# Background steps carried on into the next projection, the last shift row turned five steps later, and the first recurrence queued behind that row

## The chip, the cores and the metric

The kernel runs on one core of a Trainium2 chip. The metric is the device time of one launch in microseconds (us), lower is better. Engines are named as the profile names them: PE (TensorE matmuls), PEld (weight loads of TensorE), DVE (VectorE), ACT (ScalarE), POOL (GpSimd) and SP (SyncE, which issues most loads). Each engine works through its own instructions in the order in which they stand in its queue, and waits where an instruction needs something that another engine or a transfer has not delivered.

## The reference, cut to what matters

One decoder block on 512 tokens of width 2048, all in float32. A modulation vector is computed from `c`; the normalised input goes through one wide projection, whose columns feed attention (8 heads) and a gated recurrence, HGRN2 (8 heads).

```python
mod = silu(c) @ w_ada + b_ada
shift1, scale1, gate1, shift2, scale2, gate2 = split(mod, 6)
h = rms_norm(x, norm1_w) * (1 + scale1) + shift1
aq, ak, av, gq, gf, gi, gg = split(h @ w_in, ...)       # 7 parts of 1024 columns
attn = rms_norm(dilated_attention(rope(norm(aq)), rope(norm(ak)), av))
f = lb + (1 - lb) * sigmoid(gf)
hg = rms_norm(hgrn2(silu(gq), f, gi)) * silu(gg)         # 8 heads, a decayed running state
x = x + gate1 * (concat(attn, hg) @ w_out)
h2 = rms_norm(x, norm2_w) * (1 + scale2) + shift2
x = x + gate2 * (square(relu(h2 @ w_ff1)) @ w_ff2)
```

## The kernel before, in words

**Tiles.** Every float32 product is made of three matmuls of 128x512: both operands are split into a rounded part (`hi`, `whi`) and a rest (`lo`, `wlo`). For a weight tile ACT makes `whi` (line 39) and DVE makes `wlo` (line 40). A projection of 512 columns, `project` (L370 and on), runs over 16 steps of the contraction, called k-steps here; each k-step is 12 matmuls into four PSUM banks named `prj`. There are only four such banks, so ACT must copy a bank out (`evac`, copies at L406; `hgrn_q`, copies at L564; `hg_gate`, copies at L705) before the next projection may write to it.

**What runs beside the projections.** Two lists of generators are advanced from within `project`. After each k-step one `tick` (L360) advances the front of `tasks`: a recurrence `hgrn` of four heads with 12 ticks each, or an `attention` of four heads with 25 ticks in all. At the same place `bg_step` (L346) advances the front of `bgw`, at a rate of 2.0 steps per k-step in the first of these projections and 1.85 in the others. A background row is a matrix-vector product on DVE: `gemv` (L116) loads 16 pieces `araw` of 256 KB and adds each, times a scalar, into `acc`, one step per piece; `to_cols` (L139) then adds the two accumulators, yields, and has PE turn the row with four transposes into a bank `pc` (L149), which ACT sums up into columns (L152).

**The place of the change.** The shift vector of the first modulation is applied late: `shift_through(col0)` (L748) computes the row of `shift1 @ w_in` for columns from `col0` and adds it as a bias to values that are already there, the gates `f0` for column 4096 and the queries `hq0` for column 3072. Both rows are background steps of the projection of column 5120 (`hv0`), 32 steps in 16 k-steps, so that the transposes of the row of 3072 come with its last k-step. Then a `while bgw` loop empties the list, `bgw` is filled with `later` (a row for 4608, the four rows of `gate1`, then eight rows of the second modulation), and the first recurrence, which needs `f0`, `hq0` and `hv0`, is put on `tasks`. The projections that follow are, in order, `q0`, `k0_`, `v0`, `hq1`, `hv1`, `q1`, `k1`, `v1` and the two gates; 48 ticks of the recurrence fill exactly the 48 k-steps of `q0`, `k0_` and `v0`, and the attention of the first four heads begins with `hq1`.

**What sets the order.** On PE the order is that of the code (`manual_schedule` for PE). On the other engines a scheduler puts the instructions in order when the program is built, by the order in which the code issues them, with evacuations, weight loads, the decay levels of the recurrence and the softmax (`s_sb`, L474 to L478) put forward (`high_priority`).

**Later stages** are the output projection, the first feed-forward layer, and products of seven half-size blocks for the rest of the feed-forward layers (`product`, L1181 to L1183, whose weights DVE combines at L1149 and splits into `vlo` at L1166).

## Time and profile before

| | us |
|---|---|
| median of 3 timed runs | 2286.12 |
| lowest and highest of them | 2283.48 and 2286.8 |
| profiled execution: its span, the only time the profile gives for it | 2283.5 |
| PE busy in it | 2225.3 |
| DVE busy in it | 1809.0 |
| ACT busy in it | 1098.0 |
| projection of column 5120 (`hv0`), first to last matmul | 187.4 to 240.8 |
| last k-step of `hq1`, last matmul starts | 467.79 |

The profile counts from the first instruction to the last (the span). A row of a timeline gives start, duration, engine, line of the code, operation, "output<-inputs", shape and, in brackets, the idle time before it with what ended that. A row of the waits gives the total, the number and the longest of the waits of one kind. A row of the stretches gives for each engine its busy time and the number of its instructions, then PEclk, the share of the full TensorE clock that was granted, and the share and rate of the DMA engines.

### The profile page before, as it was taken

The page shows a single profiled execution, that of the slowest core. Times are in us where ns is not written, and L with a number is a line of the kernel's source. Part 1 is how long each engine was busy: PE and PEld are TensorE (multiplying, and loading weights), DVE is VectorE, ACT ScalarE, POOL GpSimd, SP SyncE. Part 2 cuts the span into 40 slices and gives each one's busy share as a digit, 9 for nine tenths or more (in the row PEclk, how much of TensorE's full clock was granted, in tenths as well). Part 3 has the DMA queues.
Part 4 walks back from the last instruction along what each step waited for, and adds up shares of the span by engine and source line. Part 5 has one row for each costly group of instructions (what it writes and reads, how often), then busy time and mean ns, then how long its engine had stood idle before and what let it go on. Part 6 is the DMA issues. An engine that isn't in the chain of part 4 may idle for free.

```text
span 2283.5 us, 33098 instructions
## 1 busy us (share of the span) xinstructions
PE 2225.3 (97%) x11769; PEld 1825.0 (80%) x11769; DVE 1809.0 (79%) x2765; ACT 1098.0 (48%) x1950; POOL 443.2 (19%) x664
## 2 busy tenths in 40 slices
PE   4999999999999999999999999999999999999999
PEld 3787877878778888888888888888888888788887
DVE  6999778668786575678658988998897779967878
ACT  5555434433354454447545555565564333343332
POOL 1000022000220000002232323323232222222221
PEclk9999999999999999999999999999999999999999
DMA  9798455546555266847879789789899987998784
GB/s 325 255 333 321 123 183 167 183 154 214 178 166 178 65 204 215 267 126 257 324 274 365 277 308 382 294 294 374 320 331 370 344 312 257 359 349 293 278 296 165
DMA packets 262583, 598.31 MB, mean 262 GB/s; under 512 B 23221, under 2 KB 43969, under 8 KB 262417
## 3 DMA queue, kind: packets, MB, share of 16 engines
q1 hardware_dynamic: 186800, 332.54, 43.5%
q0 software_dynamic: 70720, 254.21, 30.3%
q10 hardware_dynamic: 4896, 9.44, 1.2%
q8 instruction: 93, 1.52, 0.3%
q14 instruction: 74, 0.60, 0.1%
HBM read 518.49 MB, written 77.61 MB: 261 GB/s over the span
## 4 chain that ended last, share of the span: by engine, by line
PE 67%; issue 12%; DMA 11%; DVE 7%; POOL 3%; ACT 1%; SPq 0%; POOLq 0%; DVEq 0%; ACTq 0%
PE prj L198 9%; PE prj L200 9%; PE prj L199 8%; PE f L1183 8%; PE f L1182 8%; PE f L1181 8%; DMA f_lod<-fs 3%; PE f L208 2%; PE f L206 2%; PE f L207 2%; DMA f_hid<-part 2%; PE prj L207 2%; DVE vlo L1166 2%; PE prj L208 2%; DMA araw<-in_w_ada_dram 1%
## 5 line engine op out<-in xcount | busy, mean ns | idle before, releaser
L1165 ACT CAST vhi<-raw 128x1024 fp32r<-128x1024 f32 x392 | 413.5, 1056 | 537.9 <-PE f L1183 420.5
L1166 DVE TENSOR_TENSOR vlo<-raw,vhi 128x1024 fp32r<-128x1024 f32 x392 | 478.1, 1226 | 154.5 <-ACT vhi L1165 153.8
L1182 PE MATMUL f<-vlo,Fh 128*128 128x512 f32 x1376 | 537.7, 391 | 4.2 <-DVE vlo L1166 4.1
L1181 PE MATMUL f<-vhi,Fh 128*128 128x512 f32 x1376 | 536.9, 390 | 0.9 <-ACT vhi L1165 0.9
L1183 PE MATMUL f<-vhi,Fl 128*128 128x512 f32 x1376 | 536.3, 390 | 0.2 <-DMA Fl<-f_lod 0.2
L39 ACT CAST whi<-wraw 128x512 fp32r<-128x512 f32 (+1 forms) x368 | 220.1, 601 | 445.4 <-PE prj L200 296.0
L198 PE MATMUL prj<-whi,hi 128*128 128x512 f32 x896 | 365.1, 408 | 3.8 <-ACT gq L564 2.4
L200 PE MATMUL prj<-whi,lo 128*128 128x512 f32 x896 | 351.3, 392 | 0.0
L199 PE MATMUL prj<-wlo,hi 128*128 128x512 f32 x896 | 350.9, 392 | 0.0
L40 DVE TENSOR_TENSOR wlo<-wraw,whi 128x512 fp32r<-128x512 f32 (+1 forms) x368 | 243.8, 668 | 124.3 <-ACT whi L39 121.6
L129 DVE SCALAR_TENSOR_TENSOR acc<-araw,sc,acc 128x512 f32<-128x512 f32 (+1 forms) x392 | 253.9, 677 | 95.1 <-DMA araw<-in_w_ada_dram 94.0
L1182 PEld LDWEIGHTS f<-vlo,Fh 128*128 128x128 f32 x1376 | 258.8, 188 | 63.2 <-DVE vlo L1166 9.9
L1181 PEld LDWEIGHTS f<-vhi,Fh 128*128 128x128 f32 x1376 | 258.6, 188 | 55.0 <-ACT vhi L1165 1.4
L1183 PEld LDWEIGHTS f<-vhi,Fl 128*128 128x128 f32 x1376 | 258.8, 188 | 54.1 <-DMA Fl<-f_lod 0.6
L1149 DVE TENSOR_TENSOR raw<-raw,raw 128x1024 f32<-128x1024 f32 x224 | 269.4, 1224 | 3.4 <-DMA raw<-in_w_ff_dram 2.9
L198 PEld LDWEIGHTS prj<-whi,hi 128*128 128x128 f32 x896 | 169.0, 189 | 40.0 <-ACT gq L564 3.8
L200 PEld LDWEIGHTS prj<-whi,lo 128*128 128x128 f32 x896 | 169.0, 189 | 37.0 <-DVE lo L240 0.3
L199 PEld LDWEIGHTS prj<-wlo,hi 128*128 128x128 f32 x896 | 169.4, 189 | 32.6 <-DVE wlo L40 0.9
L1127 POOL DMA_DIRECT2D Fh<-f_hid x112 | 79.0, 705 | 428.5 <-PE f L1183 416.2
L208 PE MATMUL f<-hi,wlo 128*128 128x512 f32 x256 | 99.9, 390 | 1.5 <-DVE wlo L40 1.5
L206 PE MATMUL f<-hi,whi 128*128 128x512 f32 x256 | 100.3, 392 | 0.0
L207 PE MATMUL f<-lo,whi 128*128 128x512 f32 x256 | 99.6, 389 | 0.0
(311 smaller groups left out, 2917.2 us busy)
## 6 DMA issues: line engine op xcount, KB each, us to landing
raw<-in_w_ff_dram SPq DMA_DIRECT2D x224, 512.0 KB, 9.2
araw<-in_w_ada_dram SPq DMA_DIRECT2D x384, 256.0 KB, 4.3
Fh<-f_hid POOLq DMA_DIRECT2D x112, 512.0 KB, 6.1
Fl<-f_lod POOLq DMA_DIRECT2D x112, 512.0 KB, 7.1
wraw<-in_w_in_dram SPq DMA_DIRECT2D x104, 512.0 KB, 4.0
Fh<-h_hid POOLq DMA_DIRECT2D x60, 512.0 KB, 6.1
Fl<-h_lod POOLq DMA_DIRECT2D x60, 512.0 KB, 7.2
f_hid<-part POOLq DMA_DIRECT2D x48, 512.0 KB, 7.6
```

The costliest lines, as they stand in the source:

```text
L39: nc.scalar.copy(hi, src)
L40: (eng or nc.vector).tensor_tensor(lo, src, hi.bitcast(F32), op=ALU.subtract)
L129: dve.scalar_tensor_tensor(acc, raw[:, k - k0], vec[:, k:k + 1], acc, op0=ALU.mult, op1=ALU.add)
L198: pe.matmul(banks[ti], lhsT=hi[:, ts], rhs=whi, start=first, stop=False)
L199: pe.matmul(banks[ti], lhsT=hi[:, ts], rhs=wlo, start=False, stop=False)
L200: pe.matmul(banks[ti], lhsT=lo[:, ts], rhs=whi, start=False, stop=last)
L1149: dve.tensor_tensor(dst, a, b, op=ALU.subtract)
L1165: act.copy(hi, src)
L1166: split_done.append(dve.tensor_tensor(lo, src, hi.bitcast(F32), op=ALU.subtract))
L1181: pe.matmul(banks[t], lhsT=fh[u][a][:, ts], rhs=whi[:, a], start=first, stop=False)
L1182: pe.matmul(banks[t], lhsT=fh[u][a][:, ts], rhs=wlo[:, a], start=False, stop=False)
L1183: pe.matmul(banks[t], lhsT=fl[u][a][:, ts], rhs=whi[:, a], start=False, stop=end)
```

## The change

```diff
-    def to_cols(accs, dst):
+    def to_cols(accs, dst, lag=0):
...
             dve.tensor_tensor(accs[0], accs[0], accs[1], op=ALU.add)
-        yield
+        for _ in range(lag + 1):
+            yield
         pc = bank("pc")
...
-        yield from to_cols(gemv.acc, col[:, 0:4])
+        yield from to_cols(gemv.acc, col[:, 0:4], 5 if col0 == 3072 else 0)
...
                 forget(hd, f[h], f[h], col[:, h:h + 1])
+        shift_done.add(col0)
         yield
...
     hv0 = evac(project(5120, tok_mm, 2.0), "gi")
-    while bgw:
-        bg_step()
-    bgw[:] = later
+    bgw.extend(later)
+
+    def until(key):
+        while key not in shift_done:
+            yield
+
+    tasks.append(until(3072))
     tasks.append(hgrn(f0, hq0, hv0, hrs[0]))
```

The row of column 3072 waits five more background steps between its sum on DVE and its transposes on PE. The list is no longer emptied at the end of `hv0`, so these steps fall into `q0`: with 1.85 steps per k-step, the fifth one comes with the third k-step. A task `until` uses up the ticks until then. So on PE the transposes of that row stand three k-steps (36 matmuls) later, the first recurrence begins three ticks later, ends in `hq1` instead of `v0`, and the first attention follows three ticks later, within `hq1` and `hv1`. All background rows of `later` move by five steps, about three k-steps. From `q1` on the recurrence and the attention of the other heads stand where they stood; only the background rows still differ, until they run out. No instruction of computation is added or removed.

ACT, at the end of `hq1`, where the four `prj` banks are copied out as `gq` so that `hv1` can begin. `s_sb` are the exponentials of an attention head, `whi` weight tiles, `qT` transposed queries and keys, `sg` a gate computed from `gq`. Before:

```order
L39 CAST whi<-wraw 128x512 x2
L478 ACTIVATE s_sb,lsum<-s_sb,m 128x512
L564 COPY gq<-prj 128x512
L478 ACTIVATE s_sb,lsum<-s_sb,m 128x384
L478 ACTIVATE s_sb,lsum<-s_sb,m 128x128
L564 COPY gq<-prj 128x512
L478 ACTIVATE s_sb,lsum<-s_sb,m 128x256
L564 COPY gq<-prj 128x512
L568 ACTIVATE sg<-gq 128x512
L39 CAST whi<-wraw 128x512
L564 COPY gq<-prj 128x512
```

The same place of the changed kernel:

```order
L493 COPY p_sb<-pT 128x512 x2
L493 COPY p_sb<-pT 128x256
L565 COPY gq<-prj 128x512
L569 ACTIVATE sg<-gq 128x512
L565 COPY gq<-prj 128x512 x2
L39 CAST whi<-wraw 128x512
L569 ACTIVATE sg<-gq 128x512
L565 COPY gq<-prj 128x512
L457 ACTIVATE qT<-ptq,wcol 128x512 x2
```

The exponentials that stood around the four copies are gone from there; in their place stand the copies of the transposed weights of the same head (`p_sb`), and the next exponentials come behind the copies.

ACT, at the end of `q0`, where the four banks are copied out as `aq`. `f<-pho` copies the output of a recurrence head, `gq,hss` are the four sums of squares of it, `jk` are sums of squares of `aq`. Before:

```order
L687 COPY f<-pho 128x512
L690 ACTIVATE gq,hss<-f 128x128 x4
L39 CAST whi<-wraw 128x512 x3
L406 COPY aq<-prj 128x512
L417 ACTIVATE jk,rs_3201<-aq 128x128
L406 COPY aq<-prj 128x512
L417 ACTIVATE jk,rs_3201<-aq 128x128 x3
L406 COPY aq<-prj 128x512
L417 ACTIVATE jk,rs_3201<-aq 128x128 x4
L406 COPY aq<-prj 128x512
```

The same place of the changed kernel:

```order
L688 COPY f<-pho 128x512
L691 ACTIVATE gq,hss<-f 128x128
L407 COPY aq<-prj 128x512
L691 ACTIVATE gq,hss<-f 128x128 x3
L407 COPY aq<-prj 128x512
L418 ACTIVATE jk,rs_3106<-aq 128x128 x4
L407 COPY aq<-prj 128x512 x2
```

The output of the recurrence head now comes right ahead of the copies, three k-steps later than it did, and its squares stand between them.

DVE, early in the seven-block products of the feed-forward layer, right behind two sums `s` (L1238 before, L1244 after). `raw` is a combination of two weight tiles, `vlo` the rest part that PE waits for. Before:

```order
L1166 TENSOR_TENSOR vlo<-raw_12705,vhi 128x1024
L1149 TENSOR_TENSOR raw_12701<-raw_12709,raw_12701 128x1024
L1166 TENSOR_TENSOR vlo<-raw_12699,vhi 128x1024
L1149 TENSOR_TENSOR raw_12703<-raw_12711,raw_12703 128x1024
L1149 TENSOR_TENSOR raw_12705<-raw_12713,raw_12705 128x1024
L1149 TENSOR_TENSOR raw_12709<-raw_12717,raw_12709 128x1024
L1166 TENSOR_TENSOR vlo<-raw_12701,vhi 128x1024
L1149 TENSOR_TENSOR raw_12699<-raw_12715,raw_12699 128x1024
L1149 TENSOR_TENSOR raw_12711<-raw_12719,raw_12711 128x1024
L1149 TENSOR_TENSOR raw_12713<-raw_12721,raw_12713 128x1024
L1166 TENSOR_TENSOR vlo<-raw_12703,vhi 128x1024
```

The same place of the changed kernel:

```order
L1172 TENSOR_TENSOR vlo<-raw_12705,vhi 128x1024
L1155 TENSOR_TENSOR raw_12701<-raw_12709,raw_12701 128x1024
L1155 TENSOR_TENSOR raw_12703<-raw_12711,raw_12703 128x1024
L1172 TENSOR_TENSOR vlo<-raw_12699,vhi 128x1024
L1155 TENSOR_TENSOR raw_12705<-raw_12713,raw_12705 128x1024
L1155 TENSOR_TENSOR raw_12709<-raw_12717,raw_12709 128x1024
L1172 TENSOR_TENSOR vlo<-raw_12701,vhi 128x1024
L1155 TENSOR_TENSOR raw_12711<-raw_12719,raw_12711 128x1024
L1172 TENSOR_TENSOR vlo<-raw_12703,vhi 128x1024
```

The fourth `vlo` of this piece now stands behind five combinations instead of seven; the second stands behind two instead of one.

## The prediction

> **What bounds the kernel now.** I read the page first. Its first lines give the span and the busy time of each engine, and its list of the chain that ended last shows whose work makes up the end.

> ```profile
> span 2283.5 us, 33098 instructions
> PE 2225.3 (97%) x11769; PEld 1825.0 (80%) x11769; DVE 1809.0 (79%) x2765; ACT 1098.0 (48%) x1950; POOL 443.2 (19%) x664
> PE 67%; issue 12%; DMA 11%; DVE 7%; POOL 3%; ACT 1%; SPq 0%; POOLq 0%; DVEq 0%; ACTq 0%
> ```

> PE is busy all but 58 us. An edit that keeps its instructions can win only in those 58 us, and in stretches where PE runs slowly while it counts as busy. So the second view is the waits of PE (total, number, longest):

> ```profile
> PE pc L149 <- DVE acc L143: 4.9, 1, 4.9
> PE f L1182 <- DVE vlo L1166: 4.1, 7, 1.5
> PE prj L198 <- ACT gq L564: 2.4, 1, 2.4
> PE prj L198 <- ACT gg L705: 1.3, 1, 1.3
> ```

> Those of the first 40 us are left out here, since the change does not reach them. The 4.9 us are the transposes of the row of column 4096, inside `hv0`; I find them at 208.9 to 214.1 us. The 2.4 us end at a copy of `gq`, between `hq1` and `hv1`. The third view is the table of stretches around these waits. Behind the core's stretch stand busy times, PEclk, DMA share and rate:

> ```profile
> 208.90:214.10 5.20, 0.39 (x2) 0.00 (x0) 5.20 (x10) 0.62 (x1) 0.00 (x0) 0.74 1.06 388
> 214.10:218.20 4.10, 4.05 (x12) 3.38 (x13) 3.70 (x7) 2.84 (x7) 0.00 (x0) 0.50 1.05 387
> 467.80:470.50 2.70, 0.37 (x2) 0.00 (x0) 2.19 (x9) 1.26 (x4) 0.00 (x0) 1.00 0.03 9
> 470.50:474.20 3.70, 3.62 (x8) 2.47 (x9) 0.82 (x3) 3.70 (x12) 0.00 (x0) 0.54 0.00 0
> 809.50:813.50 4.00, 4.00 (x23) 3.44 (x24) 2.02 (x5) 3.91 (x8) 0.00 (x0) 1.00 0.47 131
> 1965.80:1969.20 3.40, 3.40 (x10) 2.66 (x9) 3.40 (x7) 0.00 (x0) 0.00 (x0) 0.50 1.04 399
> ```

> After the waits of 4.9 and 2.4 us the clock stood near half; after the 1.3 us for `gg` it did not fall. So a long wait costs more than itself.

> **The place of the edit itself: nothing to win.** Did PE wait for the row that is now turned later?

> ```profile
> 240.84 0.39 PE L200 MATMUL prj<-whi,lo 128*128 128x512 f32 x1
> 241.07 0.60 PE L149 MATMUL pc<-ident,acc 128*128 128x128 f32 x4
> 231.40 0.69 DVE L143 TENSOR_TENSOR acc<-acc 128x512 f32<-128x512 f32 x1
> ```

> No: the transposes start 0.23 us behind the last matmul of `hv0`, the normal pace, and their sum had been ready on DVE since 232. Moving them by 36 matmuls is worth 0. The distance from them to the first recurrence matmuls stays at two k-steps, so ACT and DVE have as long as before to finish the queries between them. The 4.9 us wait lies ahead of the first moved instruction; DVE, ACT, SP and PE have the same order up to there, so it stays, with its slow 4.1 us. The five lag steps issue nothing. The background rows keep their distance from their own loads; on SP the longest run of `araw` loads between two weight loads grows from seven to eleven in the new order, which the four buffers of weight loads cover as long as DVE frees the `araw` buffers in time (the slower rival below is the case where it doesn't). The three ticks are taken up by spare ones: the 25 ticks of the attention, from the fourth k-step of `hq1` on, end in the 12th of the 16 of `hv1`.

> What changes is what stands beside what at the ends of projections.

> **Term 1, the end of `hq1`.** PE, then ACT, then DVE:

> ```profile
> 467.79 0.39 PE L208 MATMUL prj<-hi,wlo 128*128 128x512 f32 x1
> 470.58 0.65 PE L198 MATMUL prj<-whi,hi 128*128 128x512 f32 x1 [2.41 <-ACT gq L564]
> 476.91 0.39 PE L199 MATMUL prj<-wlo,hi 128*128 128x512 f32 x1
> 477.82 0.39 PE L200 MATMUL prj<-whi,lo 128*128 128x512 f32 x1
> 478.05 1.25 PE L490 MATMUL pT<-ident,s_sb 128*128 128x128 f32 x10
> 469.24 0.72 ACT L478 ACTIVATE s_sb<-s_sb,m 128x512 f32<-128x512 f32 x1 [3.35 <-DVE m L477]
> 469.96 0.56 ACT L564 COPY gq<-prj 128x512 f32<-128x512 f32 x1
> 473.90 0.58 ACT L564 COPY gq<-prj 128x512 f32<-128x512 f32 x1
> 464.99 0.75 DVE L129 SCALAR_TENSOR_TENSOR acc<-araw,sc,acc 128x512 f32<-128x512 f32 x1 [1.16 <-DMA araw<-in_w_ada_dram]
> 465.66 1.92 DVE L474 SCALAR_TENSOR_TENSOR s_sb<-pscore,rs,lnc_sb 128x512 f32<-128x512 f32 x4
> ```

> ACT stood 3.35 us at an exponential that waited for DVE's maximum, and the first `gq` copy was queued behind it. DVE was late because a background piece ahead of the softmax had waited for its load. From 467.79 to 478.05 there are 25 matmul steps. At 0.2275 us each (476.91 to 477.82 is four) they take 5.69; they took 10.26. The loss is 4.6 us: 2.4 of waiting, 1.7 by the clock (3.7 us at 0.54), 0.5 of further waits for copies.

> In the changed kernel the scores of that head come at k-step 59 of the count from `q0` and those of the next at 65, while the copies come at 64, so no exponential is ahead of them. Does the new queue hold PE? Three `p_sb` copies stand ahead, and eight transposes `ptq` stand on PE before `hv1`:

> ```profile
> 478.77 1.34 ACT L492 COPY p_sb<-pT 128x512 f32<-128x512 f32 x3
> 454.52 0.60 PE L454 MATMUL ptq<-ident,aq 128*128 128x128 f32 x4
> 455.32 0.48 PE L206 MATMUL prj<-hi,whi 128*128 128x512 f32 x1
> ```

> From the start of the last k-step: `pT` began 1.0 earlier, and by the row 478.77 its copies are done 2.06 after its start, at 1.05. Then a copy (0.57), `sg`, two copies (0.47 apart, by the rows of term 2), a cast, `sg`, a copy (0.57). With 0.72 for each `sg` and the cast, what the exponential of the same width took at 469.24, the fourth bank is free at 5.3. PE ends the k-step (12 steps) at 2.7, does `ptq` in 0.8 to 0.9 and wants the fourth bank nine steps later, at 5.6. It does not wait. **-4.6 us**, between -2.4 and -4.6.

> **Term 2, the end of `q0`.** There ACT now has the output of a recurrence head just ahead of the copies. Rows of ACT, and last the wait of PE's matmuls of line 198 for `aq` (total, number):

> ```profile
> 407.89 0.59 ACT L687 COPY f<-pho 128x512 f32<-128x512 f32 x1 [1.13 <-PE pho L685]
> 408.51 0.31 ACT L690 ACTIVATE gq<-f 128x128 f32<-128x128 f32 x1
> 408.82 0.30 ACT L690 ACTIVATE gq<-f 128x128 f32<-128x128 f32 x1
> 294.55 0.57 ACT L406 COPY aq<-prj 128x512 f32<-128x512 f32 x1
> 295.02 0.31 ACT L417 ACTIVATE jk<-aq 128x128 f32<-128x128 f32 x1
>   ACT aq L406: 0.6, 2
> ```

> Again from the start of the last k-step: copy of `f` from 0.3 to 0.9, one square to 1.2, first `aq` copy to 1.7, three squares of 0.29 to 2.6, second copy to 3.1, four squares to 4.2, third copy to 4.8. PE wants the third bank at 2.7 + 1.4 = 4.1 and waits 0.7; the fourth, free at 5.3, is then in time. Before, PE waited 0.6 us in all at the two places of this kind; I take 0.2 to 0.3 of it for this one. **+0.5 us**, between 0 and +0.8; too short to fear for the clock, by the row at 809.50.

> **Term 3, the feed-forward layer.** PE waited 1.45 us for the `vlo` behind seven combinations:

> ```profile
> 1275.62 0.50 PE L1182 MATMUL f<-vlo,Fh 128*128 128x512 f32 x1 [1.45 <-DVE vlo L1166]
> 1270.94 3.50 DVE L1149 TENSOR_TENSOR raw<-raw,raw 128x1024 f32<-128x1024 f32 x3
> 1274.34 2.36 DVE L1166 TENSOR_TENSOR vlo<-raw,vhi 128x1024 fp32r<-128x1024 f32 x2
> ```

> A combination takes 1.14 (3.50 for three, overlapping). Two fewer ahead bring that `vlo` 2.3 us forward and end its wait. Two `vlo` on, one combination more stands ahead, and without the first delay PE gets there 1.5 us sooner: about 0.7 comes back. **-0.8 us**, between -1.5 and 0.

> **Sum:** -4.6 + 0.5 - 0.8 = -4.9 us on a span of 2283.5. The profile gives that execution no other time; its span equals the lowest timed run (2283.48) and lies 2.6 below the median. I take the same distance after: 2286.1 - 4.9 = **2281.2 us**.

> [...] The row 470.50 has half clock behind a wait of 2.4 us. [...]

> **Rivals.**

> *The slow clock comes anyway.* Only the waits go at the end of `hq1`, 2.9 us, and 1.7 are paid again there or at another wait. For it: the stretch at 1965.80 ran at 0.50, though no wait of a feed-forward matmul (`f`) is longer than 1.5 us by the waits. Against it: both slow stretches of this stage follow a long wait at once. -2.9 + 0.5 - 0.8 = -3.2: **2282.9**. [...] The same time comes from a smaller term 3 with a larger term 2.

> *No gain: the wait moves.* The cause of term 1 is a DVE held by loads. Its waits between 400 and 480 us, and one load in the chain of waits, start and length:

> ```profile
> DVE acc L129 <- DMA araw<-in_w_ada_dram: 11.2, 11, 2.9
> 449.31 5.37 DMA araw<-in_w_ada_dram
> ```

> DVE waited 11 times, at most 2.9 us. The exponentials now stand behind the copies but ahead of the next weight casts. If a wait there holds `whi`, 2.4 to 4.6 us come back: **2286**. Against it: in the trace the same late exponentials stood ahead of casts too, and no matmul of a projection is listed as waiting for a cast.

> *Slower: one load lands late behind the scores of k-step 65.* The longer runs on SP make this likelier than before. If a landing such as the one at 449.31 holds DVE there for its whole 5.4 us, ACT holds its casts; it decides once DVE's delay exceeds the two k-steps (5.4 us) that I take as the casts in hand. If nothing is in hand, 5.4 us of PE waiting, plus 3.4 by the clock (6.8 us at half, as from 211.4 to 218.2 around the row at 214.10), is 8.8, and against it stand the 4.9: **2290**.

> **How the numbers follow.** A measurement of this kernel can tell about 0.2%, 4.6 us, from no change. Forecast 0.46, clock anyway 0.37, no gain 0.10, slower 0.07. The forecast lies just beyond 0.2%; the second and third are within. So faster 0.46, same 0.47, slower 0.07. The low end is all of terms 1 and 3 without term 2 (-6.1) and 3 us of scatter as between the timed runs: 2277. The high end covers the third case and 2 us of scatter: 2288; it leaves out most of the slower case.

> **What would show it.** Right: no wait of PE for `gq`, PEclk 1.00 over the end of `hq1`, a wait of about 0.7 us for `aq` at the end of `q0`, the 4.9 us wait of `pc` unchanged, and the 1.45 us for `vlo` halved. Wrong: a new line with `whi` or `pc` among PE's waits between 240 and 600 us, or a half-clock stretch without a wait.

## The result and the profile after

| | before | after |
|---|---|---|
| median of 6 timed runs of each, us | 2285.93 | 2292.78 |
| lowest and highest, us | 2283.48 and 2291.61 | 2292.04 and 2296.80 |
| time of the profiled execution, us | none given | 2292.34 |
| its span, us | 2283.5 | 2290.5 |

The ratio is 1.0035, with a 95% interval of 1.0024 to 1.0046. By the medians the changed kernel is slower by 6.9 us. The forecast was 2281.2 us, its range ended at 2288, and slower had a chance of 0.07.

The first view is the waits of PE in the changed kernel between 20 and 2250 us (what, ended by which engine and line: total, number, longest). Shown are the two new ones and those that the prediction spoke of; the waits of the first 40 us, which both kernels have, are left out. From the edit on, line numbers are one higher than before, and in the feed-forward layer six.

```profile
PE pho L686 <- ACT far_sb L678: 5.1, 1, 5.1
PE pc L150 <- DVE acc L143: 4.9, 1, 4.9
PE pB L578 <- DVE z L605: 4.0, 1, 4.0
PE f L1188 <- DVE vlo L1172: 2.6, 7, 0.5
PE prj L199 <- ACT gg L706: 1.3, 1, 1.3
PE prj L199 <- ACT aq L407: 0.5, 1, 0.5
```

The 2.4 us for `gq` are gone and `aq` costs 0.5. The 1.5-us wait for `vlo` at 1275 us is gone too; the longest `vlo` wait that is left, 0.5 us at 1272.2, belongs to a matmul that stands 60 matmuls earlier in the sequence. So the three terms of the prediction came. Two long waits are new: 4.0 us for `z` and 5.1 us for `far_sb`. Both lie in the second recurrence, beside `k1` and `v1`: its level-16 matmuls `pB` want a decay product `z` of DVE, and its output matmuls `pho` want `far_sb`, ACT's copy of the scores `pE`.

The second view is the table of stretches of the changed kernel: the end of `hq1` first, then the two new waits. The columns are as in the prediction.

```profile
459.00:463.00 4.00, 4.00 (x25) 3.39 (x24) 3.01 (x5) 2.93 (x6) 0.00 (x0) 1.00 0.70 214
463.00:469.00 6.00, 6.00 (x39) 5.30 (x38) 5.16 (x10) 5.05 (x10) 0.00 (x0) 1.00 0.85 299
626.00:634.00 8.00, 4.01 (x44) 3.01 (x43) 3.76 (x10) 0.62 (x1) 0.00 (x0) 0.87 0.56 191
634.00:640.00 6.00, 6.00 (x38) 4.66 (x38) 5.95 (x18) 3.15 (x12) 1.83 (x5) 0.90 0.36 88
652.00:662.00 10.00, 4.95 (x26) 4.51 (x25) 2.81 (x6) 6.29 (x19) 1.20 (x1) 0.86 0.25 57
```

At `hq1` PE is busy throughout at full clock. Each new wait is followed by 3.4 us at half clock, from 631.8 and from 659.2, which pulls the mean PEclk of these stretches under 1.

How much each place is worth comes from a comparison of start times: the matmuls of the projections and of the feed-forward layers are the same in both kernels and come in the same sequence, so the n-th of them can be set beside the n-th.

```
matmul started (us)   before    after    after - before
last of hv0            240.8    241.1     +0.3
first of q1            526.9    523.0     -3.9
in k1                  622.9    621.4     -1.5
first of v1            636.0    639.7     +3.7   behind the wait for z
in v1                  664.6    675.7    +11.1   behind the wait for far_sb
seven-block products  1268.3   1280.3    +12.0
the same, later       1293.7   1303.9    +10.2   behind the vlo place
the same, later       1973.7   1980.5     +6.8   behind before's slow stretch of 1965.8
last                  2278.1   2285.0     +7.0
```

From the end of `hv0` to the start of `q1` PE gained 4.2 us; 0.4 of it is the four transposes of a background row, which before stand ahead of this point and after behind it. Then 2.4 went in small pieces (0.8 and 0.2 of waiting for another `z` and a `wlo`, and those 0.4; the rest is no listed wait), 5.2 at the wait for `z`, and 7.4 at the wait for `far_sb`. The last step, -3.4, is the half-clock stretch of 3.4 us from 1965.8 in before, 1.7 us lost, and 1.7 us of waiting just ahead of it (0.9 for `vhi`, 0.8 for `vlo`). After has neither, its longest wait between 1900 and 2000 us is 0.2 us; and the second profile of the order of before (the fifth run below) has no such stretch there, so it is scatter.

**Why `z` was late.** First rows of DVE in the changed kernel, last a piece of its chain of waits (start, length, what):

```profile
625.24 0.68 DVE L40 TENSOR_TENSOR wlo<-wraw,whi 128x512 fp32r<-128x512 f32 x1
629.49 0.75 DVE L129 SCALAR_TENSOR_TENSOR acc<-araw,sc,acc 128x512 f32<-128x512 f32 x1 [3.58 <-DMA araw<-in_w_ada_dram]
630.36 0.42 DVE L604 TENSOR_TENSOR z<-kk,Sx 128x256 f32<-128x256 f32 x1
631.29 0.42 DVE L605 TENSOR_TENSOR z<-gq,f 128x256 f32<-128x256 f32 x1
624.30 5.10 DMA araw<-in_w_ada_dram
```

DVE took its rows in order here: it stood 3.58 us at a running sum `acc` of a background row, whose load was issued at 624.30 and took 5.10 us, and the two halves of `z`, behind it, began at 630.36 and 631.29. Before, a sum that waited for its load stood ahead of this `z` too. Rows of DVE and then of PE, before:

```profile
625.39 0.75 DVE L129 SCALAR_TENSOR_TENSOR acc<-araw,sc,acc 128x512 f32<-128x512 f32 x1 [2.23 <-DMA araw<-in_w_ada_dram]
627.80 0.42 DVE L604 TENSOR_TENSOR z<-gq,f 128x256 f32<-128x256 f32 x1
629.20 0.46 PE L577 MATMUL pB<-z 128*32 128x32 f32 x32
```

Before, `z` was done at 628.2 and PE came for it at 629.2, with 1.0 us to spare. After, `z` was done at 631.7, 3.5 later, and PE came at 627.7, 1.5 earlier, which is what was left of the gain upstream: 1.0 - 3.5 - 1.5 = -4.0, the wait. The gain itself used up part of the slack.

**Why `far_sb` was late.** Rows of ACT, before:

```profile
646.89 0.59 ACT L677 COPY far_sb<-pE 128x512 f32<-128x512 f32 x1 [0.24 <-PE pE L676]
651.71 4.80 ACT L435 ACTIVATE ak<-ak,rs 128x128 f32<-128x128 f32 x16 [4.23 <-POOL rs L212]
```

The same piece after, with the matmul `pE` first and the power `rs` on POOL second:

```profile
649.54 1.02 PE L677 MATMUL pE<-z 128*128 128x256 f32 x4
650.19 3.02 POOL L213 TENSOR_TENSOR rs<-rs,mhalf 128x16 f32<-128x16 f32 x1 [0.44 <-DVE rs L212]
653.24 3.32 ACT L436 ACTIVATE ak<-ak,rs 128x128 f32<-128x128 f32 x11 [5.79 <-POOL rs L213]
656.97 1.56 ACT L436 ACTIVATE ak<-ak,rs 128x128 f32<-128x128 f32 x5
658.44 0.56 ACT L678 COPY far_sb<-pE 128x512 f32<-128x512 f32 x1
```

Before, the copy came first. After, the 16 scalings of the keys `ak` stand ahead of it in ACT's queue, though their factor `rs` was only ready at 653.2, and the copy, whose input was there 2.7 us before that, began at 658.44. PE came for it at 654.0 and went on at 659.1. The power took no longer than before (3.28 us then); what changed is the order.

### The profile page after: what moved, and what is told of

The parts are those of the page before. It is cut to its first block, busy times and chain, and to the rows that moved or that the text cites. A ratio compares the mean times of both kernels' runs of the same rounds, so it can differ in the third digit from the quotient of the medians.

```text
span 2290.5 us, 33088 instructions
## 1 busy us (share of the span) xinstructions
PE 2226.8 (97%) x11769; PEld 1825.9 (80%) x11769; DVE 1808.6 (79%) x2765; ACT 1099.2 (48%) x1950; POOL 441.8 (19%) x664
## 4 chain that ended last, share of the span: by engine, by line
PE 71%; DVE 12%; DMA 10%; issue 4%; ACT 2%; POOL 1%; SPq 0%; DVEq 0%; ACTq 0%; POOLq 0%
PE f L1188 11%; PE f L1189 11%; PE f L1187 11%; PE prj L199 7%; PE prj L201 7%; PE prj L200 7%; DMA araw<-in_w_ada_dram 4%; DVE vlo L1172 3%; PE f L209 2%; PE f L207 2%; PE f L208 2%; DMA Fl<-h_lod 2%; PE prj L208 2%; PE prj L207 2%; PE prj L209 2%
## 5 line engine op out<-in xcount | busy, mean ns | idle before, releaser
L199 PE MATMUL prj<-whi,hi 128*128 128x512 f32 x896 | 365.2, 408 | 1.9 <-ACT gg L706 1.3
L200 PE MATMUL prj<-wlo,hi 128*128 128x512 f32 x896 | 351.0, 392 | 0.2 <-DVE wlo L40 0.2
L129 DVE SCALAR_TENSOR_TENSOR acc<-araw,sc,acc 128x512 f32<-128x512 f32 (+1 forms) x392 | 252.7, 672 | 93.2 <-DMA araw<-in_w_ada_dram 92.2
L199 PEld LDWEIGHTS prj<-whi,hi 128*128 128x128 f32 x896 | 169.4, 189 | 38.1 <-ACT gg L706 2.1
L200 PEld LDWEIGHTS prj<-wlo,hi 128*128 128x128 f32 x896 | 169.6, 189 | 32.9 <-DVE wlo L40 0.9
L208 PE MATMUL f<-lo,whi 128*128 128x512 f32 x256 | 99.6, 389 | 0.0
```

The costliest lines, as they stand in the source:

```text
L129: dve.scalar_tensor_tensor(acc, raw[:, k - k0], vec[:, k:k + 1], acc, op0=ALU.mult, op1=ALU.add)
L199: pe.matmul(banks[ti], lhsT=hi[:, ts], rhs=whi, start=first, stop=False)
L200: pe.matmul(banks[ti], lhsT=hi[:, ts], rhs=wlo, start=False, stop=False)
```

## The experiments

Theory A: what costs is the move of the background rows by five steps, which gave DVE and ACT another order beside the second recurrence, with a late load in front of `z` and the scalings in front of `far_sb`. Theory B: the later recurrence and attention cost it. The first four kernels ran as one group; the next four and the rest on other chips, each group with its own runs of before (medians 2285.61, 2285.65, 2284.78 and 2285.49).

**Recurrence and attention moved alone.**

```diff
     bgw[:] = later
+    def idle(n):
+        for _ in range(n):
+            yield
+    tasks.append(idle(3))
     tasks.append(hgrn(f0, hq0, hv0, hrs[0]))
```

> Recurrence and attention three steps later, background rows where they stood before. Theory A (the five-step move of the background rows makes both new waits of after, the one for z behind a late araw load and the one for far_sb behind the ak scalings): neither wait is there, the gq wait of 2.4 us and its half-clock stretch are gone, 2281 to 2283 us, 3 to 5 below before. Rival B (the later recurrence and attention make them): both waits are there as in after, 2290 to 2296 us.

Measured: 2284.83 us, ratio 0.9995 (0.9986 to 1.0004). Waits of PE between 240 and 700 us:

```profile
PE pE L676 <- DVE z L604: 2.9, 1, 2.9
PE pr L180 <- DVE aq L505: 1.8, 1, 1.8
PE prj L198 <- ACT aq L406: 0.5, 1, 0.5
```

Neither wait of after is there, and the `gq` wait is gone, so B falls. But the time missed 2281 to 2283, since a 2.9-us wait with a half-clock stretch (matmuls 0.42 us apart from 375.20, against 0.23 ahead of the wait) came up in the first recurrence. Rows of ACT, DVE and PE there:

```profile
366.42 4.80 ACT L435 ACTIVATE ak<-ak,rs 128x128 f32<-128x128 f32 x16 [5.76 <-POOL rs L212]
371.76 0.69 DVE L40 TENSOR_TENSOR wlo<-wraw,whi 128x512 fp32r<-128x512 f32 x1 [1.85 <-ACT whi L39]
372.93 2.04 PE L676 MATMUL pE<-z 128*128 128x256 f32 x4 [2.88 <-DVE z L604]
```

The scalings of the first attention had waited for POOL and held a weight cast on ACT until 371.12; `wlo` waited for that cast on DVE, and `z` stood behind `wlo`.

**Background rows moved alone.**

```diff
-    bgw[:] = later
+    bgw[:] = [idle(5)] + later
```

> Background rows five steps later, recurrence and attention where they stood before. Theory A: the gq wait of before stays, and the second recurrence shows the wait for z (about 4 us with a half-clock stretch, 5.2 us in the offset) and the pho wait behind the ak scalings (about 5 us with a half-clock stretch, 7.4 us): 2295 to 2299 us, and up to 2306 if the first attention, whose scalings stand ahead of far_sb too in this order, waits in the same way. Rival B: no new wait, 2285 to 2287 us.

Measured: 2311.52 us, ratio 1.0109 (1.0093 to 1.0124). The same view:

```profile
PE pho L685 <- ACT far_sb L677: 10.5, 2, 5.8
PE pB L577 <- DVE z L604: 4.3, 1, 4.3
PE pr L180 <- DVE aq L505: 4.1, 1, 4.1
PE prj L198 <- ACT gq L564: 1.9, 1, 1.9
```

Both waits of after are there, the `far_sb` wait in both attentions, and the `gq` wait stays. The size lies above the 2306 expected: the 4.1 us for the row `gate1` (`pr`) had not been counted. The move of the background rows makes both waits, and it makes more of them when the recurrence does not move with it.

**The scalings put behind the copy.** `issue_after` puts an instruction behind another in its engine's queue.

```diff
-        act.activation(ts[ti][:, hs], ts[ti][:, hs], AF.Copy, scale=rs[:, ti, h:h + 1])
+        with tc.issue_after(far_copies[-1].ins) if far_copies else ExitStack():
+            act.activation(ts[ti][:, hs], ts[ti][:, hs], AF.Copy, scale=rs[:, ti, h:h + 1])
...
-        act.copy(far_sb[:, 2:6].rearrange("p b t -> p (b t)"), pE)
+        far_copies.append(act.copy(far_sb[:, 2:6].rearrange("p b t -> p (b t)"), pE))
```

> After with the ak scalings ordered behind the far_sb copy on ACT, nothing else moved. Theory A: the 5.1-us pho wait and its half-clock stretch go, the 4.0-us wait for z stays: 2292.8 less 7.4, about 2285.4 us. Rival C (the wait only moves, since the scalings then hold what comes behind them): 2290 to 2293 us, with a wait of the scores for ak or a later one of the recurrence in its place.

Measured: 2287.38 us, ratio 1.0008 (0.9998 to 1.0018). The three largest waits of PE between 240 and 700 us:

```profile
PE pB L579 <- DVE z L606: 3.0, 3, 2.4
PE pC L660 <- DVE z L606: 0.9, 1, 0.9
PE pC L654 <- DVE z L606: 0.7, 1, 0.7
```

The `far_sb` wait is gone: over its place the offset against before grows by 0.4 us, where after had 7.4. But 2.0 us are lost in the next head of the recurrence, mostly at the two waits for `z` in front of `pC`. So C falls in its size and holds in this smaller part. By the medians 5.4 us came back where 7.4 were expected. Two more things moved with the new order: the wait for `z` at 628 us is 2.4 us here, not 4.0, and no half-clock stretch follows it, and the `vlo` wait is back at 1.4 us, since the order of DVE in the feed-forward layer turned to that of before.

**Both put right.** As above, and for the second recurrence:

```diff
+    zs = []
...
-                    dve.scalar_tensor_tensor(acc, raw[:, k - k0], ...)
+                    with tc.issue_after(zs[-1].ins) if zs else ExitStack():
+                        dve.scalar_tensor_tensor(acc, raw[:, k - k0], ...)
...
+            if any(f is t for t in f1) and L in (16, 32):
+                zs.append(zi)
```

> As the run before it, and in the second recurrence the running sums of the background rows stand behind the z products of levels 16 and 32 on DVE. Theory A with its part on z (z is late because DVE, which works in order, stands at a sum whose araw load is late): the wait for z and its half-clock stretch go too, 2285.4 less 5.2, about 2280 us. Rival D (z is late for another reason, or the sums held back make the loads behind them late in turn): a wait of 2 us or more stays between 600 and 680 us, 2284 us or more.

Measured: 2282.23 us, ratio 0.9990 (0.9981 to 0.9999). All waits of PE between 240 and 700 us:

```profile
PE pE L683 <- DVE z L609: 0.7, 1, 0.7
PE prj L202 <- ACT aq L410: 0.5, 1, 0.5
```

And DVE at the place of the late `z`:

```profile
622.40 0.41 DVE L609 TENSOR_TENSOR z<-gq,f 128x256 f32<-128x256 f32 x1
622.74 0.68 DVE L625 TENSOR_TENSOR mt<-pA,hgm 128x128 f32<-128x128 f32 x3
623.34 1.40 DVE L132 SCALAR_TENSOR_TENSOR acc<-araw,sc,acc 128x512 f32<-128x512 f32 x2
```

`z` stands ahead of the sums, and these find their loads landed. D falls. Two changes of order that remove no work make the changed kernel 10.6 us faster by the medians (9.3 by the median of a second group of runs below).

**The lag at zero.** After, with `0` for the `5`.

> After with the lag of the last shift row at 0 in place of 5 and all else of the change kept. If the five idle steps are the whole of what moves, every engine's rows stand as in before, and it takes as long as before, 2285 to 2287 us, with the gq wait and the 1.45-us vlo wait back. If carrying the background rows on or holding the recurrence behind the row costs something of its own, it lies above. Its profile is at the same time a second look at the order of before: vlo waits that differ from before's 4.1 us by as much as after's 2.6 us did are scatter between executions and no effect of the change.

Measured: 2285.19 us, ratio 1.0000 (0.9991 to 1.0010), with the `gq` wait (2.8 us) and the longest `vlo` wait (1.5 us) back. Carrying the list on and holding the recurrence behind the row cost nothing that shows; the five idle steps are the effect. That the `vlo` waits are scatter, the other thing this run was to show, falls: DVE's order at 1275 us decides. With the order of before there, in eleven profiles, the wait was 1.4 to 1.5 us; with that of after, in two, there is none over 0.15 us at this matmul; with a third order, in two more, at most 0.5.

**The sums alone put behind `z`.**

> After with only the sums of the background rows behind the z products of levels 16 and 32 in the second recurrence; the ak scalings are left to stand ahead of far_sb (9 of the 16 in this order). Theory A: the wait for z goes and the pho wait of 4 to 5 us with its half-clock stretch stays: 2292.8 less 5.2, 2287 to 2288 us. Rival D: the wait for z stays in another place, 2290 us or more.

Measured: 2289.80 us, ratio 1.0016 (1.0006 to 1.0027). The wait for `pB` is gone and that for `far_sb` is 3.8 us. The mechanism is as expected, the time 2 to 3 us above; the `vlo` waits total 6.1 us here, against 2.6 in after (the profile is that of the slowest of the ten runs).

**A lag of 2 and of 3 steps.** After, with `2` or `3` for the `5`.

> After with a lag of 2 steps in place of 5. In this order far_sb stands ahead of the 16 ak scalings of the second attention, as in before, and the gq copies stand free, as in after. Theory A, with the losses a matter of where the background rows fall and not of the change itself: no pho wait and no gq wait; whether a sum holds z depends on which loads are late, so 2281 us without a wait for z and up to 2286 with one. If any later row or recurrence costs the same as five steps do: about 2290 us or more.

> After with a lag of 3 steps in place of 5; far_sb stands ahead of the ak scalings of the second attention here too. Theory A as for a lag of 2: no pho wait, no gq wait, 2281 us without a wait for z and up to 2286 with one. If a later row or recurrence costs the same as five steps do: about 2290 us or more.

Measured: 2290.00 us, ratio 1.0019 (1.0005 to 1.0032), and 2290.56 us, ratio 1.0028 (1.0018 to 1.0039). Waits with a lag of 2:

```profile
PE pB L578 <- DVE z L605: 4.9, 3, 3.8
PE pho L686 <- ACT far_sb L678: 0.3, 1, 0.3
```

And with a lag of 3:

```profile
PE pB L578 <- DVE z L605: 6.7, 4, 2.7
PE pho L686 <- ACT far_sb L672: 0.3, 1, 0.3
```

The times are those of the case set against theory A, about 2290, so they alone don't decide. The waits do: there is no long `far_sb` wait, as the order said, but a wait for `z` is there, and it costs more than the upper end I gave (2286). It does not need five steps: lags of 2, 3 and 5 have it, the lag of 0 has not. With a lag of 3 its longest piece falls at 588 us, in an earlier head. And these two kernels gained less upstream, 2.5 and 0.8 us from the end of `hv0` to the start of `q1`, where after gained 4.2; why is open. That the lag itself costs nothing once `z` is free is shown by the lag of 2 with the sums behind `z`, below.

**More buffers for the loads.** After, with `bufs=5` or `6` for the 4 of `araw`, and 29 or 28 for the 30 of the pool `io`.

> After with 5 buffers for the araw loads of the background rows in place of 4 (one buffer less in the pool io, 29 for 30). The scalings stay ahead of far_sb, so the pho wait of 5 us with its half clock is expected in every case. Theory A1 (the late load is late because it is issued only when a sum four loads earlier has set its buffer free): the wait for z shrinks from 4.0 us to under 2 and loses its half-clock stretch, about 2288 us. Theory A2 (the loads are late because the DMA engines are full there): the wait stays near 4 us, about 2293 us.

> The same with 6 buffers (28 in the pool io). Theory A1: no wait for z over 1 us, about 2287 to 2288 us, the rest being the pho wait. Theory A2: the wait stays near 4 us, about 2293 us.

Measured: 2290.85 us, ratio 1.0033 (1.0023 to 1.0043), and 2296.79 us, ratio 1.0052 (1.0037 to 1.0066). The longest waits for `z`, with 5 and with 6 buffers:

```profile
PE pB L578 <- DVE z L605: 4.8, 2, 3.9
PE pB L578 <- DVE z L605: 4.4, 2, 4.1
```

The wait stays, so more buffers are no cure. They did not bring the load earlier, and A1 is not settled by that: DVE stood 2.88 us at a load that SP issued at 623.29 with 5 buffers and at 629.22 with 6, and each time a sum had ended less than 0.05 us before. So a sum still held the issue. With 6, PE was 4.3 us behind before already at the matmul of 241 us, where with 5 it was 2.0 ahead; this kernel lost time of its own there, perhaps by the smaller pool `io`.

**The lag of 2, with the sums behind `z`.**

> The lag of 2 steps with the sums of the background rows behind the z products of levels 16 and 32 in the second recurrence. With a lag of 2 the only new wait was that for z, 3.8 us with a half-clock stretch, 5.7 us in the offset. Theory A: it goes, 2290.0 less 5.7, about 2284 us, and near the 2282 of the fourth experiment. Rival D (holding the sums back only moves the wait): 2287 us or more.

Measured: 2285.07 us, ratio 0.9998 (0.9989 to 1.0007). No wait for `pB` above 0.9 us. The 3.8-us wait went and no long one came in its place, as in the fourth run; the time is 1.1 us above the expected one.

**Half the bytes in each load.** In the rows beside the second recurrence `m` is half of `n`.

```diff
-            nc.sync.dma_start(raw, view[:, k0:k0 + nk, col0:col0 + n])
+            nc.sync.dma_start(raw[:, :, 0:m], view[:, k0:k0 + nk, col0:col0 + m])
...
+                    r = raw[:, k - k0:k - k0 + 1, 0:m].broadcast_to([P, 2, m])
```

> After with half the bytes in each araw load of the rows that run beside the second recurrence (128 KB for 256): they read the first 256 columns of each 512 and their sums use these twice, so the gates and the second modulation are not those of the reference, while every sum works on as many elements as before. The scalings stay ahead of far_sb, so the pho wait of 5 us is expected in every case. Theory A2 (the loads come late because too many bytes are asked for at once): the wait for z goes, about 2287 to 2288 us. Theory A3 (they come late because of the order of issues on SP, whatever their size): a wait for z of 3 us or more stays, 2291 to 2293 us.

Measured: 2287.83 us, ratio 1.0008 (0.9999 to 1.0018). Waits, and the loads between 612 and 632 us (KB each, median us to landing):

```profile
PE pho L691 <- ACT far_sb L683: 4.7, 1, 4.7
PE pB L583 <- DVE z L610: 1.9, 1, 1.9
araw<-in_w_ada_dram SPq DMA_DIRECT2D x9, 128.0 KB, 2.8
```

In after the same view has 11 loads of 256 KB and 4.7 us, in before 8 loads of 256 KB and 3.0 us. The wait at 628 us is gone; one of 1.9 us, with half clock behind it, ended at 584.8 instead. The time is that of A2, but DVE's order differs in this kernel too, and before shows that the size of a load alone does not make it late.

The traces tell what does. SP issues these loads and the 512-KB weight loads `wraw` on one queue. In the 15 profiles, between 560 and 640 us, 279 `araw` loads were issued while a weight load was under way, and all 279 landed after that weight load (22 of them in before, 16 in after). In after these took 4.65 us (median), the others 2.73; with half the bytes it is 3.45 and 2.12. The load at which DVE stood in after was issued at 624.30, half a microsecond behind a weight load that landed at 627.93, and landed at 629.40. So the place on SP counts, as A3 has it, and the bytes count too.

**The fourth kernel once more.**

> The kernel of the fourth experiment once more: after with both orders put right, the scalings behind far_sb on ACT and the sums behind the z products on DVE. If it is faster than before and not only so in that group of runs: 2281 to 2284 us, 1 to 4 below before in the same group, with no PE wait over 1 us between 240 and 700 us. If not: within 1 us of before.

Measured: 2283.50 us, ratio 0.9993 (0.9984 to 1.0002), with the same two short waits as the fourth. Over the two groups, 22 runs have a mean of 2283.74 us and the 48 runs of before beside them 2285.66. The difference is 1.9 us with a standard error of 0.55: faster than before, but by less than 0.1%.

## Why the prediction was wrong

- **The place of the edit: 0.** Right. At the end of `hv0` the two kernels differ by 0.3 us, and the kernel with the lag at zero takes as long as before. The 4.9-us `pc` wait stayed.
- **Terms 1 and 2, the ends of `hq1` and `q0`: -4.6 + 0.5 = -4.1.** Right in mechanism and size: no `gq` wait, PEclk 1.00, 0.5 us of waiting for `aq` (0.7 forecast), and 3.8 us gained from the end of `hv0` to the start of `q1` once the 0.4 of the row that is turned later are set aside.
- **Term 3, the `vlo`: -0.8.** Right in mechanism; the 1.5-us wait is gone and its place is worth 1.8 in the offset. Against that stand 1.0 us lost shortly ahead of it, 0.5 of them the `vlo` wait at 1272.2. That the net, -0.7, comes so near to the forecast is in part luck, since the prediction had the small loss behind the place and not ahead of it.
- **The step that failed** is the sentence "The background rows keep their distance from their own loads", by which the move of these rows was costed at nothing except in the slower rival. It speaks of the distance between a row and its load; what mattered was the distance between a row and the recurrence on the same engine. What stood at nothing in the sum measured 5.2 us at the wait for `z` and 7.4 us at the wait for `far_sb`, both in the second recurrence. The prediction compared orders at the ends of `q0` and `hq1` and in the feed-forward layer, and left out `k1` and `v1` between them; the statement that recurrence and attention stand where they stood from `q1` on holds for PE and not for DVE and ACT. Both losses could have been sought there: one is a scaling that moved ahead of a copy in ACT's order, which the order shows, the other needed the slack of 1.0 us at `z`, which the trace of before shows.
- **The rival "one load lands late"** had the first link of one of the two waits right, DVE in order behind a late load, and the half clock at the end. Its middle was another: it went by casts that ACT holds, where in fact PE stood at DVE's `z` itself. It was placed at the scores of k-step 65, where nothing happened, and got 0.07; that its 2290 lies near the measured time is luck. The `far_sb` wait, the larger one, was in no rival.
- **The range.** The low end assumed that terms gained stay gained. They were gained, and still the best kernel with both waits put right is 1.9 us below before, not 4.9: the term at the `vlo` is absent in it, since the reordering turned that order back, and of the 4 us gained at `q1` some 2 are lost again by 860 us in it too (offset -3.4 and -1.3 in one profile of it, -4.3 and -2.0 in the other), with no wait over 1.3 us.

Open: how far the late loads beside the second recurrence are due to their place behind a weight load and how far to a sum that holds their issue, and why the scheduler put the scalings ahead of the copy.

## What to carry to other kernels

A gain upstream brings PE earlier to everything downstream, so the slack of each later hand-over (ready time against the time PE asks for it) has to be read from the trace before a gain is counted. When background work moves relative to a chain of small dependent steps, compare the new order of every engine over the whole stretch in which both run, and look for two patterns: a piece with a load in front of a product that PE wants, and a batch that waits for a slow engine in front of a copy that PE wants. Putting the urgent instruction ahead in these two queues was worth 9 to 11 us here without any change of the work. A small load that shares a queue with large ones is a third thing to look at: here each of the 279 that were issued while a weight load was under way landed after it.

## What was not expected of the hardware

I cut each of them into windows of this length, counted from such a start, and added up the time in which no matmul ran (gaps over 0.15 us, with 0.23 us for a matmul). After 100 us and up to the last 7, all 52 windows that were idle for 0.60 or more of their length were followed by a window at half clock. Of the 98 with 0.30 to 0.57, 96 were not; the two others lie within a slow stretch that had already begun. At half clock the slower pace itself counts as idle in this sum; with the windows at full clock alone it is 37 of 37, and 0 of 65. Of these, before has 3 of 3 (from 207.9, 467.4 and 1962.4 us, idle for 0.65, 0.75 and 0.62) and 0 of 1, after 3 of 3 (from 208.6, 628.4 and 655.7, idle for 0.83, 0.98 and 0.97) and 0 of 4. The nearest cases:

```
run                        window from (us)   idle share   next window
fourth kernel again            1242.4            0.57       full clock
half the bytes                  647.1            0.57       full clock
6 buffers                       655.8            0.60       half clock
rows moved alone                483.4            0.60       half clock
half the bytes                  582.2            0.62       half clock
before                         1962.4            0.62       half clock
```

These are counts of the 15 traces and no more. A stretch of 3.413 us at half clock takes about 1.7 us from PE (an estimate: half its length, at a PEclk of 0.50), and in these runs a wait cost that on top of itself or not by where it fell: 2.0 us idle within one window slowed PE at 585.7 in the kernel with half the bytes, while 2.4 us across two windows (0.3 and 0.4 of them) did not in the kernel with the scalings moved. The 2.4-us wait of before fell with other idle time into the window from 467.4, idle for 0.75. The stretch at 1965.80 of the prediction, which had no long wait ahead of it, fits these counts too: stretches of before, with the slow one second.

```profile
1962.40:1965.80 3.40, 1.71 (x7) 0.89 (x6) 1.75 (x3) 1.04 (x1) 0.00 (x0) 1.00 1.05 394
1965.80:1969.20 3.40, 3.40 (x10) 2.66 (x9) 3.40 (x7) 0.00 (x0) 0.00 (x0) 0.50 1.04 399
```

The first was idle in two short waits, 0.93 us for `vhi` and 0.76 for `vlo`, and in all for half of its time by this view and for 0.62 at 0.23 us a matmul.
